# Four converted and five raw weight chunks in place of five and three, and a pool of their own for the bias tiles, in one decoder layer

## The chip, the cores and the metric

The kernel runs on one core of one Trainium2 chip, in one launch. The metric is the device time of one execution in microseconds, as the median of several runs. The profile shows the engines as PE (TensorE matmul), PEld (its weight load), DVE (VectorE), ACT (ScalarE), POOL (GpSimd) and SP (SyncE, which here only starts transfers).

## The reference

One layer of a decoder on 256 tokens of width 2048, all in float32:

```python
h  = rms_norm(x, norm_mix_pre)
c_q, c_kv, k_r, q_s, k_s, v_s, gates = split(h @ w_in)          # 2048 -> 7488
q  = rms_norm(c_q) @ w_q_up ; kv = rms_norm(c_kv) @ w_kv_up
A  = latent attention (16 heads, causal, rotary part)
B  = banded attention (32 query heads, 4 key heads, window 128,
     sinks, bias = rel_table[t5_bucket(distance)])
y  = (sigmoid(gA) * (A @ w_o_mla) + sigmoid(gB) * (B @ w_o_swa)) @ w_out
x  = x + rms_norm(y, norm_mix_post)
h  = rms_norm(x, norm_ffn_pre)
a, b = split(h @ w_up)                                           # 2048 -> 2 x 5632
y  = (gelu(causal_conv3(a)) * b) @ w_down
x  = x + rms_norm(y, norm_ffn_post)
```

## The kernel before

Every product of activations and weights is made of three matmuls on numbers split in a high and a low part (`fp32r`): high x high, high x low, low x high (`mm3`, L147 to L149, and the same in the FFN's first product at L977 and L981). The 256 tokens are two row blocks, t = 0 and t = 1.

The weights come in chunks of up to 1024 columns of a [128, 1024] tile, 512 KB each, 501 in all. A chunk has three steps (`wchunk`): SP loads it into a raw tile (L119), ACT copies it to the high part `whi` (L121), DVE subtracts that from the raw tile and gets the low part `wlo` (L122). Raw tiles come from a ring of `RAW` buffers (3) and are free when `wlo` is done; the pairs `whi`, `wlo` come from rings of `RING` buffers each (5) and are free when the last matmul has read them. So the load of chunk n waits for the `wlo` of chunk n - RAW, and the `whi` of chunk n for the matmuls of chunk n - RING. A tile takes 4 KB of each partition. A chunk may be given a pool of its own (`own`).

`gemm` runs over the chunks of one block of up to 512 output columns. With 512 columns a chunk holds two k-tiles, which makes 6 matmuls for each row block; with 256 columns it holds four k-tiles and makes 12 shorter ones for each. With `split=True` the matmuls of t = 1 are put aside in `todo` and run after those of t = 0 of the whole block, so that the work on the first rows can start while PE does the second rows. Then every chunk of the block stays converted until its turn in `todo`. This is used three times: in the last block of W_out (eight chunks, 229 to 236, the first three in a pool `px` with `EXTRA` = 3 buffers, the other five in the ring), in the first block of the FFN's product (chunks 237 to 244: one in pool `p8`, three in `px`, four in the ring), and in the last block of W_down (five chunks, 496 to 500, all in the ring).

Behind the last block of W_out stands `resid(t)`: the sum of squares (`yj`, `vy`), the inverse root in small steps (`ry`), `x2 = yg * ry + x2` (L840), transposes (`x2T`, L843) and the split into the FFN's input (`bhl`, L847 on ACT and L850 on DVE). Behind the last block of W_down stand `z_evac` (`z`, L1037 and `zj`, L1039) and `finish` (a root on ACT, L1054, and `ds`, L1062, with the stores) for each row block in turn.

The banded attention works in 16 units of two heads. Each loads its bias, 384 distances for each of two heads, from a strip in DRAM by two transfers of POOL (L425, L426) and adds it to the scores (L437, L438). Its queries come through `qx` (L203), transposes `xp` (L403) and a copy `x` (L406).

The order of the instructions on an engine is set by the Tile framework's scheduler at build time, with steps tied to the chunk number by `at` and `tick`; the first product's ACT, DVE and SP instructions stay in the order of the code. An engine takes its instructions in that order. Pools are taken from the on-chip memory one above the other: a pool that is opened after another was closed lies in the same place, and the first writer there waits for the last reader of what was there. `p1` takes the place of `p0`.

Of the kernel before, what the change touches and what calls it, by code (L numbers as in the profile page):

```python
# [19 lines left out]
P = 128  # L20
# [21 lines left out]
def trunk_layer(ctx, tc, x, x_cols_in, conv_cols_in, g_mix_post, g_ffn_post, w_in, w_q, w_kv,  # L42
# [4 lines left out]
    def open_pool(name, bufs=1, **kw):  # L47
        es = ExitStack()
        return es, es.enter_context(tc.tile_pool(name=name, bufs=bufs, **kw))
# [6 lines left out]
    base = ctx.enter_context(tc.tile_pool(name="base", bufs=1))  # L56
    ring = ctx.enter_context(tc.tile_pool(name="ring", bufs=RING))

    def sb(pl, shape, name, dt=F32, tag=None, bufs=None):
        return pl.tile(shape, dt, name=name, tag=tag or name, **({"bufs": bufs} if bufs else {}))  # L60
# [43 lines left out]
    def wchunk(src, shape, own=None, rawp=None, rbufs=1):  # L104
# [3 lines left out]
        raw = rawp.tile([P, 1024], F32, name=f"raw{i}", tag="xraw", bufs=rbufs) if rawp else \  # L108
            ring.tile([P, 1024], F32, name=f"raw{i}", tag="raw", bufs=RAW)
        dst = raw[:, :n]  # L110
# [26 lines left out]
    def drain():  # L137
        while steps:
            tick()
# [65 lines left out]


    esl, lpool = open_pool("lpool")
    es0, p0 = open_pool("p0")

    gx = sb(p0, [P, 38 + 256], "gx")  # L210
# [132 lines left out]
    es1, p1 = open_pool("p1")  # L343
# [72 lines left out]
    def swa_unit(u, t0):  # L416
# [3 lines left out]
        st = {}  # L420

        def load():
            st["bias"] = sb(p1, [P, 2, 384], f"bias{u}", tag="bias", bufs=2)
            row = lambda n: bass.AP(strip.tensor, strip.offset + h0 * 384, [[1, P], [384, 2], [1, n]])
            pool.dma_start(st["bias"][:, :, 0:256], row(256))  # L425
            pool.dma_start(st["bias"][:, :, 256:384], row(128))  # L426
            st["p"] = sb(p1, [P, 2, 384], f"p{u}", tag="p", bufs=3)
            st["mx"] = sb(p1, [P, 2, 2], f"mx{u}", tag="mx", bufs=3)
# [45 lines left out]
        def pv():  # L474
# [16 lines left out]
            pool.tensor_tensor(OL(u), st["o"], OH(u).bitcast(F32), op=ALU.subtract)  # L491

        at(t0 - (3 if u > 1 else 1), load)
        at(t0, lambda: score(0), lambda: score(1))
        at(t0 + 1, stats, lambda: expo(0), lambda: expo(1), norm)
# [99 lines left out]
    tb = {0: gate_b(0), 1: gate_b(1)}  # L595
    drain()
    es1.close()


    es2, p2 = open_pool("p2")  # L600
# [482 lines left out]
    es3.close()  # L1083


RING = 5
XCUT = [0, 1, 2, 3, 4, 6, 8, 10, 12, 14, 16]
X_LOAD = [0, 1, 2, 3, 4, 6, 7, 8, 10]
X_SQ = [4, 4, 5, 5, 6, 7, 8, 9, 10, 11]
# [3 lines left out]
LINE_B = 80  # L1093
LINE_W = 64
LINE_Z = 48
RAW = 3
STG = 4


# [61 lines left out]
```

## Time and profile before

| | |
|---|---|
| median of 3 runs | 1485.72 us (1485.46 to 1486.3) |
| the profiled execution: time | 1489.58 us |
| the profiled execution: span | 1487.8 us |
| mean granted TensorE clock | 0.997 |
| PE, DVE, ACT busy | 99%, 66%, 54% of the span |
| read from memory | 277.79 MB, 191 GB/s over the span |

The profile is of one execution on the one core; times in it are microseconds from the start of its span. A row of the timeline gives start, duration, engine, line, operation and tiles (without their numbers), and in brackets the idle time of the engine before it and what ended that. A row of the waits gives who waited for what: microseconds in all, times, the longest.

### The profile page before, as it was taken

To read this page: it belongs to the slowest core of one execution; us is meant where nothing else is said; L and a number is where in the kernel's file an instruction comes from. 1 tells how busy PE (TensorE), PEld (TensorE's weight loads), DVE (VectorE), ACT (ScalarE), POOL (GpSimd) and SP (SyncE) were. 2 spreads that over 40 slices of the span, in tenths; PEclk is the share of its full clock that TensorE was granted. 3 is DMA by queue.
4 is the path that set the end of the run, shared out by engine and by line. 5 is a ranking of instruction groups with operands and counts; after the bars stand their busy time and mean duration, and the time that the engine had idled before them with its cause. 6 is when DMAs were issued, how large, how long until landed. Compare 5 with 4: busy or idle time off the path is not lost.

```text
span 1487.8 us, 21191 instructions
## 1 busy us (share of the span) xinstructions
PE 1472.7 (99%) x7797; PEld 1263.0 (85%) x7797; DVE 979.4 (66%) x1711; ACT 806.0 (54%) x1336; POOL 57.9 (4%) x97
## 2 busy tenths in 40 slices
PE   9999999999999999999999999999999999999997
PEld 7788888888899988888888888888888888888887
DVE  7688884444667765555698776676444676677555
ACT  7588874434555554444566555554444555555443
POOL 0122210000000001000000000000000000000000
PEclk9999999999999999999999999999999999999999
DMA  8676656666655559766656666665556666665563
GB/s 268 191 192 156 166 174 199 211 206 206 184 157 162 164 162 307 245 216 201 198 171 184 198 187 183 198 187 189 191 196 197 187 185 191 190 189 184 194 196 114
DMA packets 162324, 285.52 MB, mean 192 GB/s; under 512 B 18555, under 2 KB 34844, under 8 KB 162092
## 3 DMA queue, kind: packets, MB, share of 16 engines
q1 hardware_dynamic: 157436, 268.39, 58.5%
q0 software_dynamic: 4784, 15.78, 4.2%
q8 instruction: 61, 1.00, 0.3%
q14 instruction: 43, 0.35, 0.1%
HBM read 277.79 MB, written 6.34 MB: 191 GB/s over the span
## 4 chain that ended last, share of the span: by engine, by line
PE 90%; ACT 3%; DMA 3%; DVE 3%; issue 1%; SPq 0%; DVEq 0%; ACTq 0%
PE accg L148 17%; PE accg L149 17%; PE accg L147 17%; PE ub L977 10%; PE ua L977 10%; PE ua L981 5%; PE ub L981 5%; DMA raw<-in_w_in_dram 3%; ACT whi L121 1%; ACT p L455 1%; DVE wlo L122 1%; PE mpo L730 1%; PE ms L696 1%; PE qn L659 1%; PE qn L660 1%
## 5 line engine op out<-in xcount | busy, mean ns | idle before, releaser
L122 DVE TENSOR_TENSOR wlo<-raw,whi 128x1024 fp32r<-128x1024 f32 (+2 forms) x501 | 608.6, 1217 | 421.3 <-ACT whi L121 420.1
L121 ACT CAST whi<-raw 128x1024 fp32r<-128x1024 f32 (+2 forms) x501 | 523.4, 1046 | 544.7 <-PE accg L149 305.7
L147 PE MATMUL accg<-whi,bhl 128*128 128x512 f32 (+1 forms) x608 | 230.9, 380 | 0.0
L149 PE MATMUL accg<-whi,bhl 128*128 128x512 f32 (+1 forms) x608 | 230.1, 378 | 0.0
L148 PE MATMUL accg<-wlo,bhl 128*128 128x512 f32 (+1 forms) x608 | 230.0, 378 | 0.0
L147 PE MATMUL accg<-whi,ahl 128*128 128x512 f32 (+1 forms) x544 | 213.3, 392 | 0.0
L148 PE MATMUL accg<-wlo,ahl 128*128 128x512 f32 (+1 forms) x544 | 210.9, 388 | 0.0
L149 PE MATMUL accg<-whi,ahl 128*128 128x512 f32 (+1 forms) x544 | 210.7, 387 | 0.0
L977 PE MATMUL ub<-ahl,whi 128*128 128x512 f32 x640 | 160.4, 392 | 0.0
L977 PE MATMUL ua<-ahl,whi 128*128 128x512 f32 x640 | 160.2, 392 | 0.0
L977 PEld LDWEIGHTS ua<-ahl,whi 128*128 128x128 f32 x640 | 115.7, 189 | 21.1
L977 PEld LDWEIGHTS ub<-ahl,whi 128*128 128x128 f32 x640 | 115.5, 189 | 21.1 <-ACT cc L897 0.2
L149 PEld LDWEIGHTS accg<-whi,bhl 128*128 128x128 f32 x608 | 114.4, 188 | 21.4
L148 PEld LDWEIGHTS accg<-wlo,bhl 128*128 128x128 f32 x608 | 114.4, 188 | 20.9
L147 PEld LDWEIGHTS accg<-whi,bhl 128*128 128x128 f32 x608 | 114.4, 188 | 20.9
L149 PEld LDWEIGHTS accg<-whi,ahl 128*128 128x128 f32 x544 | 102.4, 188 | 20.5
L147 PEld LDWEIGHTS accg<-whi,ahl 128*128 128x128 f32 x544 | 102.5, 188 | 18.0
L148 PEld LDWEIGHTS accg<-wlo,ahl 128*128 128x128 f32 x544 | 102.6, 189 | 17.7
L981 PEld LDWEIGHTS ub<-ahl,wlo 128*128 128x128 f32 x640 | 86.3, 191 | 5.6
L981 PEld LDWEIGHTS ua<-ahl,wlo 128*128 128x128 f32 x640 | 86.0, 191 | 5.5
L981 PE MATMUL ub<-ahl,wlo 128*128 128x256 f32 x640 | 88.0, 282 | 0.0
L981 PE MATMUL ua<-ahl,wlo 128*128 128x256 f32 x640 | 87.9, 282 | 0.0
(331 smaller groups left out, 1621.6 us busy)
## 6 DMA issues: line engine op xcount, KB each, us to landing
raw<-in_ffn_w_up_dram SPq DMA_DIRECT2D x176, 512.0 KB, 4.5
raw<-in_w_in_dram SPq DMA_DIRECT2D x111, 512.0 KB, 4.6
raw<-in_ffn_w_down_dram SPq DMA_DIRECT2D x88, 512.0 KB, 4.1
raw<-in_w_o_swa_dram SPq DMA_DIRECT2D x32, 512.0 KB, 3.9
raw<-in_w_o_mla_dram SPq DMA_DIRECT2D x32, 512.0 KB, 4.8
raw<-in_w_out_dram SPq DMA_DIRECT2D x32, 512.0 KB, 4.1
raw<-in_mla_w_q_up_dram SPq DMA_DIRECT2D x48, 128.0 KB, 2.7
bias<-strip POOLq DMA_DIRECT2D x16, 256.0 KB, 3.9
```

What stands on the lines that cost most here:

```text
L121: act.copy(hi[:, :n], raw[:, :n])
L122: vec.tensor_tensor(lo[:, :n], raw[:, :n], hi[:, :n].bitcast(F32), op=ALU.subtract)
L147: pe.matmul(o, ah, bh, start=start, stop=False)
L148: pe.matmul(o, ah, bl, start=False, stop=False)
L149: pe.matmul(o, al, bh, start=False, stop=stop)
L455: act.activation(pb[:, i, a:b], pb[:, i, a:b], AF.Exp, bias=st["nm"][:, i, t:t + 1], accum_out=st["sm"][:, i, t:t + 1])
L659: pe.matmul(o, wh, ch(k), start=k == 0, stop=False)
L660: pe.matmul(o, wh, cl(k), start=False, stop=False)
L696: pe.matmul(o, w, v_, start=n == 0, stop=False)
L730: pe.matmul(o, w(t), p_[:, c], start=n == 0, stop=n == 5)
L977: pe.matmul(acc[i], hi[:, c], hn[p][:, j * 512:(j + 1) * 512], start=p + j == 0, stop=stop)
L981: pe.matmul(acc[i][:, 0:256], lo[:, c], hn[p][:, j * 512:j * 512 + 256], start=False, stop=False)
```

## The change

Two sizes and one pool:

```diff
     esl, lpool = open_pool("lpool")
+    esb, pbias = open_pool("pbias")
     es0, p0 = open_pool("p0")
...
-            st["bias"] = sb(p1, [P, 2, 384], f"bias{u}", tag="bias", bufs=2)
+            st["bias"] = sb(pbias, [P, 2, 384], f"bias{u}", tag="bias", bufs=2)
...
     es1.close()
+    esb.close()
...
-RING = 5
+RING = 4
...
-RAW = 3
+RAW = 5
```

The ring of pairs loses one `whi` and one `wlo` tile (8 KB of a partition), the raw ring gains two tiles (8 KB). The two bias buffers (3 KB each) no longer lie in `p1`, above what `p0` held in the head, but in a place that nothing has used before. Lines after L207 move down by one, those after L598 by two.

The scheduler's order stays the same in nearly all places, with one difference throughout: where the conversion of chunk n + 1 stood, that of chunk n stands now. Three places differ by more or matter here.

ACT, in the head, ahead of the copy of the first transposed queries (`x20`; `qx`, `vx`, `kx` are the attention's queries, values and keys). Before:

```order
L121 CAST whi21_771<-raw21_769 128x1024
L121 CAST whi22_809<-raw22_807 128x1024
L200 CAST vx0_567<-vr0_615 128x4x64
L121 CAST whi23_863<-raw23_861 128x1024
L200 CAST vx1_568<-vr1_637 128x4x64
L200 CAST kx0_563<-kt0_641 128x384
L406 CAST x20_652<-xp0_647 128x512
L406 CAST x21_664<-xp1_659 128x512
```

ACT in the same place, after:

```order
L121 CAST whi20_723<-raw20_721 128x1024
L121 CAST whi21_774<-raw21_772 128x1024
L200 CAST vx0_570<-vr0_618 128x4x64
L121 CAST whi22_812<-raw22_810 128x1024
L200 CAST vx1_571<-vr1_640 128x4x64
L200 CAST kx0_566<-kt0_644 128x384
L407 CAST x20_655<-xp0_650 128x512
L407 CAST x21_667<-xp1_662 128x512
```

The last conversion ahead of `x20` is chunk 22's in place of chunk 23's; the rest is the same.

DVE, between W_out and the FFN, in the inverse root for the first rows (`vy0`, `ry0`), up to the first of `x2_0`. Before:

```order
L837 TENSOR_SCALAR vy0_7154<-vy0_7154 128x1
L179 TENSOR_SCALAR ry0_y_7157<-vy0_7154 128x1
L182 SCALAR_TENSOR_TENSOR ry0_t_7158<-vy0_7154,ry0_y_7157 128x1
L189 TENSOR_SCALAR ry0_t_7158<-ry0_t_7158 128x1
L190 TENSOR_TENSOR ry0_y_7157<-ry0_y_7157,ry0_t_7158 128x1
L182 SCALAR_TENSOR_TENSOR ry0_t_7158<-vy0_7154,ry0_y_7157 128x1
L122 TENSOR_TENSOR wlo238_7370<-raw238_7367,whi238_7369 128x1024
L192 TENSOR_SCALAR ry0_u_7159<-ry0_t_7158 128x1
L193 TENSOR_TENSOR ry0_u_7159<-ry0_u_7159,ry0_t_7158 128x1
L122 TENSOR_TENSOR wlo239_7382<-raw239_7379,whi239_7381 128x1024
L194 SCALAR_TENSOR_TENSOR ry0_y_7157<-ry0_u_7159,ry0_y_7157 128x1
L840 SCALAR_TENSOR_TENSOR x2_0_0_5855<-yg_0_0_6558,ry0_y_7157,x2_0_0_5855 128x512
```

DVE in the same place, after (eight more small steps of both rows, without a `wlo`, follow before `x2_0_0`):

```order
L828 TENSOR_TENSOR yg_0_3_6565<-accg_229_0_7057,gpost_5870 128x512
L839 TENSOR_SCALAR vy0_7158<-vy0_7158 128x1
L179 TENSOR_SCALAR ry0_y_7161<-vy0_7158 128x1
L122 TENSOR_TENSOR wlo242_7422<-raw242_7419,whi242_7421 128x1024
L182 SCALAR_TENSOR_TENSOR ry0_t_7162<-vy0_7158,ry0_y_7161 128x1
L122 TENSOR_TENSOR wlo243_7434<-raw243_7431,whi243_7433 128x1024
L189 TENSOR_SCALAR ry0_t_7162<-ry0_t_7162 128x1
L838 TENSOR_REDUCE vy1_7279<-ssy1_6571 128x1
L828 TENSOR_TENSOR yg_1_3_6569<-accg_229_1_7058,gpost_5870 128x512
L190 TENSOR_TENSOR ry0_y_7161<-ry0_y_7161,ry0_t_7162 128x1
L839 TENSOR_SCALAR vy1_7279<-vy1_7279 128x1
L122 TENSOR_TENSOR wlo244_7446<-raw244_7443,whi244_7445 128x1024
```

Three conversions of later chunks (242 to 244) now stand among these small steps in place of 238 and 239, and steps of the second rows (`vy1`, `yg_1_3`) as well. On PE, in the same place, the last six matmuls of t = 0, those of chunk 236, moved behind 30 and 34 of the 48 of t = 1.

PE, in the last block of W_down (`accg_496_0` is t = 0, `accg_496_1` is t = 1). Before:

```order
L147 MATMUL accg_496_0_13785<-whi500_13861,ghl9_7565 128x256
L148 MATMUL accg_496_0_13785<-wlo500_13862,ghl9_7565 128x256
L149 MATMUL accg_496_0_13785<-whi500_13861,ghl9_7565 128x256
L147 MATMUL accg_496_1_13786<-whi496_13789,bhl0_7556 128x256
L148 MATMUL accg_496_1_13786<-wlo496_13790,bhl0_7556 128x256
L149 MATMUL accg_496_1_13786<-whi496_13789,bhl0_7556 128x256
```

PE in the same block, after, with 22 matmuls of t = 1 ahead of the first row of chunk 500:

```order
L147 MATMUL accg_496_1_13790<-whi497_13811,bhl3_7563 128x256
L147 MATMUL accg_496_0_13789<-whi500_13865,ghl8_7568 128x256
L148 MATMUL accg_496_1_13790<-wlo497_13812,bhl3_7563 128x256
L149 MATMUL accg_496_1_13790<-whi497_13811,bhl3_7563 128x256
L147 MATMUL accg_496_1_13790<-whi498_13829,bhl4_7564 128x256
L148 MATMUL accg_496_1_13790<-wlo498_13830,bhl4_7564 128x256
L149 MATMUL accg_496_1_13790<-whi498_13829,bhl4_7564 128x256
L147 MATMUL accg_496_1_13790<-whi498_13829,bhl4_7564 128x256
L148 MATMUL accg_496_1_13790<-wlo498_13830,bhl4_7564 128x256
L149 MATMUL accg_496_1_13790<-whi498_13829,bhl4_7564 128x256
L147 MATMUL accg_496_1_13790<-whi498_13829,bhl5_7565 128x256
L148 MATMUL accg_496_0_13789<-wlo500_13866,ghl8_7568 128x256
```

Before, t = 1 follows when t = 0 is complete; now the twelve matmuls of chunk 500 for t = 0 stand in the middle of those of t = 1.

## The prediction

> **What bounds the kernel now.** I read the page's first lines, then the waits, then one window of the long middle.
>
> ```profile
> PE 1472.7 (99%) x7797; PEld 1263.0 (85%) x7797; DVE 979.4 (66%) x1711; ACT 806.0 (54%) x1336; POOL 57.9 (4%) x97
> PE 90%; ACT 3%; DMA 3%; DVE 3%; issue 1%; SPq 0%; DVEq 0%; ACTq 0%
> L122 DVE TENSOR_TENSOR wlo<-raw,whi 128x1024 fp32r<-128x1024 f32 (+2 forms) x501 | 608.6, 1217 | 421.3 <-ACT whi L121 420.1
> L121 ACT CAST whi<-raw 128x1024 fp32r<-128x1024 f32 (+2 forms) x501 | 523.4, 1046 | 544.7 <-PE accg L149 305.7
> ```
>
> PE is busy for 1472.7 of 1487.8 us, so all that can be won inside the span is about 15 us, and the change has to be priced where PE stands still or comes to stand still. The two conversions of a chunk take 1.05 us on ACT and 1.22 us on DVE.
>
> ```profile
> ACT whi L121 <- PE accg L149: 305.7, 198, 2.5
> ACT whi L121 <- DMA raw<-in_w_o_mla_dram: 29.3, 14, 4.1
> ACT whi L121 <- DMA raw<-in_w_in_dram: 24.1, 23, 3.9
> SPq L119 <- DVE wlo L122: 854.0, 360, 11.1
> 300.00:350.00 50.00, 50.00 (x222) 41.42 (x221) 23.25 (x20) 21.12 (x21) 1.08 (x2) 1.00 0.65 205
> ```
>
> ACT mostly waits for PE to give back a converted pair (305.7 us in 198 waits): the conversions run ahead as far as the ring lets them. Waits of ACT for the raw data are a sixth of that. The loads on SP wait 854.0 us for wlo, which frees a raw buffer. From 300 to 350 us PE is busy for 50.00 of 50.00 us (second number of the window's row), so none of these waits costs anything there. What counts is the few places where PE stops: the head, where the first weights come in, the handover from W_out to the FFN, and the end.
>
> **The steady stages: nothing.** A pair is freed four chunks ahead of its use with five pairs, and three ahead with four. A chunk is 12 matmuls of 512 columns; 48 such matmuls take the 10.88 us from 719.63 to 730.51 in the rows on the handover below, 0.227 us each, so a chunk is 2.72 us. The lead shrinks from 4 x 2.72 = 10.9 us to 8.2 us, of which the conversions need 1.05 + 1.22 = 2.3 us. About 5.9 us stay as cover for other work of ACT and DVE in between. The extra two raw buffers take away ACT's waits for raw data (29.3 and 24.1 us), which PE did not feel. Bounds: -2 us, if some of PE's 15 us without work goes with them, and +2 us, if in the banded attention, where ACT and DVE have most other work, the cover is used up once. I take 0.
>
> **The bias pool: nothing.** The first bias load no longer waits for what lay in that memory before, only for its source.
>
> ```profile
> POOL bias L425 <- DMA raw<-in_w_in_dram: 5.3, 1, 5.3
> 67.80 0.29 DVE L437 TENSOR_TENSOR p<-s,bias 128x128 f32<-128x128 f32 x1 [4.04 <-PE s L435]
> ```
>
> At most 5.3 us of waiting on POOL go, but the first reader, at 67.80, waited last for PE's scores and not for the bias. The scores hide it.
>
> **The head: a gain of 3.3 us.** Here a stall of PE does hang on the raw data.
>
> ```profile
> 54.69 1.05 ACT L121 CAST whi<-raw 128x1024 fp32r<-128x1024 f32 x1 [3.87 <-DMA raw<-in_w_in_dram]
> ...
> 60.66 1.04 ACT L121 CAST whi<-raw 128x1024 fp32r<-128x1024 f32 x1 [1.15 <-DMA raw<-in_w_in_dram]
> ...
> 62.24 0.60 ACT L406 CAST x<-xp 128x512 fp32r<-128x512 f32 x1
> 58.07 0.40 PE L149 MATMUL accg<-whi,ahl 128*128 128x512 f32 x1
> 60.46 0.40 PE L147 MATMUL accg<-whi,ahl 128*128 128x512 f32 x1
> 62.89 0.75 PE L403 MATMUL xp<-ident_r,qx 128*128 128x128 f32 x4 [2.03 <-ACT x L406]
> 63.44 0.76 PE L148 MATMUL accg<-wlo,ahl 128*128 128x512 f32 x1
> ...
> 66.11 0.39 PE L148 MATMUL accg<-wlo,ahl 128*128 128x512 f32 x1
> 64.00:66.00 2.00, 2.00 (x6) 1.61 (x5) 0.00 (x0) 0.27 (x1) 0.00 (x0) 0.50 0.91 271
> ```
>
> ACT takes its instructions in order. The x copy, for which PE stands still for 2.03 us, is behind the conversion at 60.66 (chunk 23), which waited 1.15 us for its load, as the one at 54.69 had waited 3.87. After the stall the granted clock is 0.50 (the third number from the end of the window's row, with the busy share of the DMA engines and the GB/s behind it), and from 63.44 to 66.11 six matmuls take 2.67 us in place of 6 x 0.227 = 1.36: another 1.3 us. With five raw buffers the load of chunk n waits for the wlo of chunk n-5 and no longer n-3, two conversions earlier, and with one pair less the conversion in that place of the row is chunk 22's. What gates it is the pair of chunk 18, whose last matmul is the one at 58.07, done at 58.5. So it starts 2.2 us earlier than 60.66. The x copy keeps its distance of 1.58 us: 60.1. The transposes at 62.89 follow 0.65 us behind it, at 60.7, where PE comes free at 60.9 (60.46 + 0.40). The stall goes, and the lower clock with it: -2.03 - 1.3 = -3.3. Bounds: 0, if the loads come no earlier because the DMA queues are what limits here (0.91 of them are busy from 64 to 66), and -3.6. I take the far end, since the gate that is left is a row of PE's and not a transfer.
>
> **The handover from W_out to the FFN: +5.9 us and something for the clock.** The last block of W_out runs all its matmuls for the first 128 rows (t0) and then those for the others (t1), so every chunk of it stays converted until its t1 matmuls come. Eight chunks, 229 to 236: three have buffers of their own, five fill the ring of five. In a ring of four, chunk 236 has to wait for chunk 232's t1.
>
> ```profile
> 719.63 0.39 PE L147 MATMUL accg<-whi,ahl 128*128 128x512 f32 x1
> ...
> 730.51 0.39 PE L147 MATMUL accg<-whi,ahl 128*128 128x512 f32 x1
> ...
> 736.89 1.34 PE L843 MATMUL x2T<-ident,x 128*128 128x128 f32 x8
> ...
> 743.80 0.39 PE L147 MATMUL accg<-whi,bhl 128*128 128x512 f32 x1
> 730.77 0.60 ACT L825 ACTIVATE yj<-accg 128x512 f32<-128x512 f32 x1 [3.88 <-PE accg L149]
> ...
> 732.07 1.05 ACT L121 CAST whi<-raw 128x1024 fp32r<-128x1024 f32 x1 [0.61 <-PE accg L149]
> ...
> 737.55 2.17 ACT L847 ACTIVATE bhl<-x2T,gmat 128x128 fp32r<-128x128 f32 x8 [1.70 <-PE x2T L843]
> 733.31 1.22 DVE L122 TENSOR_TENSOR wlo<-raw,whi 128x1024 fp32r<-128x1024 f32 x1
> ...
> 734.71 1.23 DVE L122 TENSOR_TENSOR wlo<-raw,whi 128x1024 fp32r<-128x1024 f32 x1
> ...
> 736.03 2.74 DVE L840 SCALAR_TENSOR_TENSOR x<-yg,ry_y,x 128x512 f32<-128x512 f32 x4
> ...
> 739.83 2.15 DVE L850 SCALAR_TENSOR_TENSOR bhl<-x2T,gmat,bhl 128x128 fp32r<-128x128 f32 x8
> ```
>
> Before, t0 is complete at 730.7 (yj at 730.77). The norm of its rows on DVE (two wlo stand in it), x at 736.03, the transposes at 736.89 and the splits behind them all run while PE does t1, and the FFN's first matmul at 743.80 waits for nothing. In the new order 42 matmuls of t0 are in a row, then t1 starts (719.63 + 42 x 0.227 = 729.15), and t0's last six stand behind 30 and 34 of t1's. Chunk 232 is free after t1's 24th, at 734.8 with its drain; whi 236 runs 734.8 to 735.9, wlo to 737.1, and t0 is complete at 738.5, or 7.8 us later. On DVE the norm of these rows now has three wlo in it (242, 243, 244), each behind a whi that waits for a pair that t1 still reads: 234 is free at 738.9, 235 at 740.3, 236 at 741.6. Adding 1.05 and 1.22 to these: wlo 242 ends at 741.5, 243 at 742.8, 244 at 744.9, and with the small steps left x starts at 745.65 and the first transposes at about 746.5. PE has no matmul left after 741.45 (48 + 48 done). The first k-tiles of the FFN's input, transposed, scaled and split, come at about 749.0, with eight more transposes (0.7 us) to do then: 749.0 + 0.7 - 743.80 = +5.9. If no wlo stood in that chain, the first transposes would come at 742.2 and the price would be +0.8: that is the lower bound. I take the upper one, since DVE can't overtake its own row.
>
> For the clock, the head's rows say that 2.03 us without work were followed by 0.50 until 66.11 and cost 1.3 us. Here PE is idle for about 5 us, cut by transposes of 128 columns, of which I can't say whether they keep the clock up. Between 0 and 1.3 I take the middle, +0.6. [...]
>
> **The tail: +2.9 us.** The last block of W_down is split in the same way and has five chunks, 496 to 500, all in the ring.
>
> ```profile
> 1464.60 0.28 PE L147 MATMUL accg<-whi,bhl 128*128 128x256 f32 x1
> ...
> 1471.80 0.28 PE L147 MATMUL accg<-whi,bhl 128*128 128x256 f32 x1
> ...
> 1478.88 0.28 PE L149 MATMUL accg<-whi,ghl 128*128 128x256 f32 x1
> 1464.80 1.05 ACT L121 CAST whi<-raw 128x1024 fp32r<-128x1024 f32 x1 [1.83 <-PE accg L149]
> ...
> 1473.05 1.28 ACT L1054 ACT_TABLE_LOAD   x1
> 1472.00 0.42 DVE L1037 TENSOR_TENSOR z<-ds,accg 128x256 f32<-128x256 f32 x1 [4.58 <-PE accg L149]
> ...
> 1475.51 2.74 DVE L1062 SCALAR_TENSOR_TENSOR ds<-ds,rz,x 128x512 f32<-128x512 f32 x4
> 1479.20 0.42 DVE L1037 TENSOR_TENSOR z<-ds,accg 128x256 f32<-128x256 f32 x1 [0.95 <-PE accg L149]
> ...
> 1481.36 2.74 DVE L1062 SCALAR_TENSOR_TENSOR ds<-ds,rz,x 128x512 f32<-128x512 f32 x4
> ```
>
> t0 and t1 are 60 matmuls of 0.12 us each (7.20 us from 1464.60 to 1471.80). Before, the first rows finish while t1 runs: z at 1472.00, table load, small steps, ds until 1478.25, and then DVE idles 0.95 us for t1. In the new order t0 stops after 48 (1470.36). whi 500 waits for chunk 496's t1 (12 matmuls, 1.44 us, and the drain: 1472.05), ends at 1473.1, wlo at 1474.4. t0's last eleven stand behind 31 of t1's and end at 1475.9, so z of the first rows comes 3.9 us later. The work behind it takes 1478.2 - 1472.0 = 6.2 us on DVE, and z of the other rows stands behind it: 1475.9 + 6.2 = 1482.1 in place of 1479.20, +2.9. All after that is one chain to the last store. PE's own end moves by 0.2 us at most. Bounds: 0, if t0 were no more than 0.95 us late, and +3.2.
>
> **Sum.** -3.3 + 5.9 + 0.6 + 2.9 = +6.1 us. The profiled execution's span is 1487.8 and its time 1489.58, 3.9 us above the runs' median; a difference carries over: 1485.72 + 6.1 = 1491.8 us.
>
> **The rivals.** (a) No difference that a measurement of this kernel can tell (within 0.2%, 2.97 us): the handover is cheap, +0.8, because the norm's small steps aren't held up by the three wlo. For it: with two wlo in it that norm still took only 5.3 us (730.77 to 736.03). Against it: the releases that these wlo now wait for lie behind t1. Time: 1485.72 - 3.3 + 0.8 + 2.9 = 1486.1.
> (b) Faster: the deeper raw ring is worth more than its place in the head. Of PE's 15 us without work some in the banded attention go too; with -3.3 in the head, -2 there, the handover at +0.8 and a tail of +1 it is 1482.2. It decides if the handover stays under about +1.3. Against it: the whole middle shows no idle PE, and the attention's short stalls are behind ACT and DVE rather than loads.
> (c) Slower by more: PE starves where cover is thinnest (+2, the bound above), the head gains nothing, or the clock falls fully: 1491.8 + 0.7 + 2 = 1494.5, and 1497.8 with no gain in the head.
>
> **Chances.** My case 0.60, (c) 0.16, (a) 0.14, (b) 0.10. Slower by over 0.2% (above 1488.7): mine and (c), 0.76. Faster (below 1482.7): 0.10. The range leaves out (b) and the worst of (c): 1485 to 1496. My case's own range is 1489 to 1494.
>
> **What would show it.** Right: PE's 2.03 us at 62.89 and the 0.50 clock behind it are gone; a PE stall of about 5 us shows just ahead of the FFN's first matmul with x2T waited for; yj of the first rows about 7.8 us later against the start of t1; the last z waits for DVE and not for PE. Wrong: no stall at the handover (then whi 236 got its pair earlier than I count), or stalls of PE on wlo in the banded attention.

## The result and the profile after

The changed kernel takes 1496.7 us (median of 4 executions, 1496.28 to 1496.94), the kernel before 1486.01 us (4 executions, 1485.46 to 1486.89): a ratio of 1.0071, 95% interval 1.0054 to 1.0089. That is 10.7 us more, where 6.1 were forecast and the range ended at 1496 us. The direction, the two places of the loss and most of their sizes came out; the gain in the head did not come, and the clock's term was too small.

First the head, in the timeline of the changed kernel (ACT, then PE), and the same place in a second profile of the kernel before, which has a span of 1484.3 us.

```profile
58.37 1.04 ACT L121 CAST whi<-raw 128x1024 fp32r<-128x1024 f32 x1 [1.81 <-PE accg L149]
...
59.95 0.60 ACT L407 CAST x<-xp 128x512 fp32r<-128x512 f32 x1
60.33 0.40 PE L147 MATMUL accg<-whi,ahl 128*128 128x512 f32 x1
60.61 0.53 PE L404 MATMUL xp<-ident_r,qx 128*128 128x128 f32 x4
```

```profile
58.57 1.05 ACT L121 CAST whi<-raw 128x1024 fp32r<-128x1024 f32 x1 [0.83 <-PE accg L149]
...
60.16 0.60 ACT L406 CAST x<-xp 128x512 fp32r<-128x512 f32 x1
60.49 0.40 PE L147 MATMUL accg<-whi,ahl 128*128 128x512 f32 x1
60.81 0.37 PE L403 MATMUL xp<-ident_r,qx 128*128 128x128 f32 x2
64.00:66.00 2.00, 2.00 (x18) 1.69 (x17) 1.68 (x8) 1.31 (x3) 0.00 (x0) 1.00 0.16 60
```

After the change the conversion ahead of the x copy waits for PE's pair, starts at 58.37 (58.5 was forecast), and PE runs through. But in the second profile of the kernel before it does so too: 58.57, waiting for PE, x at 60.16, the transposes right behind the matmul at 60.49, and a granted clock of 1.00 from 64 to 66. The stall that the prediction meant to win was not there to be won in that execution.

Then the handover, changed kernel: ACT, DVE and PE, and four windows (the granted clock is the third number from the end).

```profile
731.09 1.06 ACT L121 CAST whi<-raw 128x1024 fp32r<-128x1024 f32 x1 [0.30 <-PE accg L149]
...
734.97 0.60 ACT L827 ACTIVATE yj<-accg 128x512 f32<-128x512 f32 x1 [1.47 <-PE accg L149]
736.63 1.22 DVE L122 TENSOR_TENSOR wlo<-raw,whi 128x1024 fp32r<-128x1024 f32 x1
...
737.91 1.22 DVE L122 TENSOR_TENSOR wlo<-raw,whi 128x1024 fp32r<-128x1024 f32 x1
...
739.90 1.21 DVE L122 TENSOR_TENSOR wlo<-raw,whi 128x1024 fp32r<-128x1024 f32 x1
...
741.86 0.75 DVE L842 SCALAR_TENSOR_TENSOR x<-yg,ry_y,x 128x512 f32<-128x512 f32 x1
715.93 0.39 PE L147 MATMUL accg<-whi,ahl 128*128 128x512 f32 x1
...
742.71 1.94 PE L845 MATMUL x2T<-ident,x 128*128 128x128 f32 x8 [4.65 <-issue]
744.53 0.79 PE L147 MATMUL accg<-whi,bhl 128*128 128x512 f32 x1
...
747.05 0.63 PE L148 MATMUL accg<-wlo,bhl 128*128 128x512 f32 x1
740.00:742.00 2.00, 0.00 (x0) 0.00 (x0) 2.00 (x10) 0.00 (x0) 0.53 (x1) 0.53 0.85 249
742.00:744.00 2.00, 1.29 (x6) 1.20 (x7) 2.00 (x5) 1.23 (x3) 0.00 (x0) 0.50 0.99 304
...
748.00:750.00 2.00, 2.00 (x8) 1.64 (x7) 1.10 (x2) 0.98 (x5) 0.00 (x0) 0.50 0.08 29
750.00:752.00 2.00, 2.00 (x11) 1.60 (x10) 1.13 (x4) 1.50 (x7) 0.00 (x0) 0.91 0.00 0
```

W_out's last block begins at 715.93 (719.63 in the execution that the prediction read). The conversion of chunk 236 at 731.09 waits for PE, the sum of squares of the first rows (yj) follows at 734.97, the three subtractions stand in the norm's chain, and x starts at 741.86. PE, idle for 4.65 us, is then at half clock (0.50 in every window from 742 to 750) until about 750.

Last the tail, DVE of the changed kernel:

```profile
1480.80 0.42 DVE L1039 TENSOR_TENSOR z<-ds,accg 128x256 f32<-128x256 f32 x1 [1.68 <-PE accg L149]
...
1484.29 2.74 DVE L1064 SCALAR_TENSOR_TENSOR ds<-ds,rz,x 128x512 f32<-128x512 f32 x4
1486.95 0.41 DVE L1039 TENSOR_TENSOR z<-ds,accg 128x256 f32<-128x256 f32 x1
```

The second z has no wait in brackets any more: it stands behind the first rows' ds on DVE, where before it waited 0.95 us for PE.

How much each stretch costs can be read from the first matmul of W_out's last block and the first of W_down's last block. The second profile of the kernel before has these at

```profile
716.19 0.39 PE L147 MATMUL accg<-whi,ahl 128*128 128x512 f32 x1
...
1461.13 0.28 PE L147 MATMUL accg<-whi,bhl 128*128 128x256 f32 x1
```

and the changed kernel has the first at 715.93 (above) and the second at

```profile
1469.42 0.28 PE L147 MATMUL accg<-whi,bhl 128*128 128x256 f32 x1
```

Up to W_out's last block the changed kernel is 0.3 us ahead. From there to W_down's last block it takes 753.49 us in place of 744.94, which is 8.55 more, and from there to the end of the span 25.7 in place of 23.2, which is 2.5 more. Together that is 10.8, the difference of the two spans (1495.1 and 1484.3).

### The profile page after: what moved, and what is told of

Its sections match the earlier page's. It is cut to its first block, busy times and chain, and to the rows that moved or that the text cites. A ratio compares the mean times of both kernels' runs of the same rounds, so it can differ in the third digit from the quotient of the medians.

```text
span 1495.1 us, 21182 instructions
## 1 busy us (share of the span) xinstructions
PE 1474.7 (99%) x7797; PEld 1263.5 (85%) x7797; DVE 979.9 (66%) x1711; ACT 807.3 (54%) x1336; POOL 57.1 (4%) x97
## 4 chain that ended last, share of the span: by engine, by line
PE 93%; DVE 4%; ACT 2%; issue 1%; DMA 0%; SPq 0%; DVEq 0%; ACTq 0%
PE accg L149 17%; PE accg L147 17%; PE accg L148 17%; PE ub L979 10%; PE ua L979 10%; PE ua L983 5%; PE ub L983 5%; DVE wlo L122 1%; PE mpo L732 1%; PE ms L698 1%; ACT p L456 1%; PE qn L661 1%; PE qn L663 1%; PE qn L662 1%; PE acckv L148 0%
```

## The experiments

**The kernel before, again.** No edit.

> The unchanged kernel, profiled again. Theory A: the 2.03 us stall of PE in the head and the half clock behind it belonged to the one profiled execution that the prediction read, which was 3.9 us above the median of the runs; ordinary executions don't have them, so the change has nothing to win there. Then the span is about 1484 us (3.5 less than 1487.8), the conversion ahead of the x copy waits for no transfer, and PE runs through from 55 to 66 us at full clock. Theory B: every execution has the stall, and the 3.9 us are spread elsewhere: span near 1484 too, but with the 2.03 us and the clock of 0.50 at 64 us in it.

Measured: 1486.09 us, ratio 0.9998 (0.9988 to 1.0007). The profiled span is 1484.3 us, and all ten executions have spans between 1483.6 and 1484.9; 25 more of the same kernel on that chip lie between 1483.6 and 1485.5. The execution of the prediction (1487.8) is outside of all of them (the longest span of this kernel in any later run is 1486.8), and the rows above show the head without its stall. PE's rows of the two traces are together up to 58 us (the matmul at 58.07 stands at 58.09 here) and 3.4 us apart behind the stall (the `kt` transposes at 74.94 and 71.51), as they still are at W_out's last block (719.63 and 716.19). So the head makes nearly all of the 3.5 us by which that execution was longer, and theory A holds for these two. Two traces of later runs with the same rings, of the bias pool alone and of `EXTRA = 2` (both below), show a stall of 0.30 us and none in that place, at a granted clock of 1.00. Why the loads came later in the one execution is not shown, and of the executions without a trace only the spans are known.

**The handover's cause undone.** Chunk 236 gets a pair outside the ring; the FFN's first chunks trade places:

```diff
-extra={i: (px,) for i in range(EXTRA)} if last else None)
+extra={i: (px,) for i in range(EXTRA)} | {7: (p8,)} if last else None)
...
-first_extra = {0: (p8,)} | {i + 1: (px,) for i in range(EXTRA)}
+first_extra = {i: (px,) for i in range(EXTRA)} | {EXTRA: (p8,)}
```

> The changed kernel, with the handover's cause undone alone: chunk 236 gets the buffers of pool p8 and chunk 237 and 240 trade places with it, so that W_out's last block needs four pairs of the ring. The trace of the changed kernel puts the loss there at about 8.3 us (stall and clock). A: 1496.7 - 8.3 = 1488.4 us, PE's 48 matmuls of the first rows in a row and no stall ahead of the FFN. B (the handover's loss is only the forecast 6.5, the rest of the miss is elsewhere): 1490.2.

**The tail's cause undone.** The last block's fifth chunk uses two tiles that nobody reads any more:

```diff
+class Free:
+    def tile(self, shape, dt, name, tag):
+        return base.tile(shape, dt, name=name, tag="ahl0" if tag == "whi" else "ahl1")
...
-return gemm(xh, xl, w_down, k0, nk, c0, n, split=split, ps=ps)
+return gemm(xh, xl, w_down, k0, nk, c0, n, split=split, extra={4: (Free(),)} if split else None, ps=ps)
```

> The changed kernel, with the tail's cause undone alone: the fifth chunk of W_down's last block gets two tiles that nothing reads any more, so that the block needs four pairs of the ring. Both theories: 1496.7 - 2.9 = 1493.8 us, the last z waits for PE again. If it stays above 1495.7, the tail's term is under 1 us and its place is elsewhere.

**Both undone.** The two edits together.

> Both undone, so that the ring of four, the raw ring of five and the bias pool are left without a block that needs a fifth pair. A (nothing to win in the head): 1496.7 - 8.3 - 2.9 = 1485.5 us, the same as before within 1 us. B (the head's 3.3 us are won in every execution): 1482.7 us.

Measured: handover undone 1490.05 us (ratio to before 1.0027, 1.0018 to 1.0037), tail undone 1493.54 us (1.0047, 1.0032 to 1.0062), both 1487.17 us (1.0010, 1.0001 to 1.0020). Against 1496.7 that is -6.65, -3.2 and -9.5 us. The tail is near what was expected. Its four executions lie between 1492.07 and 1494.82 us, so the 3.2 is a rough figure; the step from the handover alone to both is 2.9. The last z waits for PE again (DVE, tail undone):

```profile
1484.88 0.42 DVE L1043 TENSOR_TENSOR z<-ds,accg 128x256 f32<-128x256 f32 x1 [0.95 <-PE accg L149]
```

The handover gives less than the 8.3 expected, and 1490.05 is the number that theory B gave. That is by chance. PE's timeline of that run shows why: no stall ahead of the FFN, the transposes between W_out's matmuls, but a new wait that the edit itself brought, since chunk 240 now waits for chunk 236's pair.

```profile
733.39 1.32 PE L845 MATMUL x2T<-ident,x 128*128 128x128 f32 x8
...
745.96 0.50 PE L148 MATMUL accg<-wlo,bhl 128*128 128x512 f32 x1 [1.24 <-DVE wlo L122]
```

With its 1.24 us the handover is worth 7.9 us by the medians, where the rows of the two blocks above gave 8.55; B's 6.5 is too little. The run with both undone has the same wait (1.23 us), which is most of the 1.7 us that it lies above A's 1485.5.

**Both undone, without that wait.** Pool p8 goes to the FFN's chunk 244 in place of 240:

```diff
-first_extra = {i: (px,) for i in range(EXTRA)} | {EXTRA: (p8,)}
+first_extra = {i: (px,) for i in range(EXTRA)} | {7: (p8,)}
```

> Both blocks undone as in the combined run, with a better place for the FFN's chunks: pool p8, which chunk 236 now uses, goes to chunk 244 (needed last) in place of 240, and 240 to 243 use the ring. The 1.23 us that PE waited for chunk 240's subtraction should go: 1487.2 - 1.2 to 1.6 = 1485.8 us, no difference from before (1486.0). If the deeper raw ring is worth something in ordinary executions once the blocks fit, it is below 1484; if the shorter ring costs something in the steady stages, it stays at 1487.

Measured: 1485.55 us against 1486.89 of before, ratio 0.9993 (0.9984 to 1.0002): no difference that is clear of the measurement, and about 11 us faster than the changed kernel. The wait is gone, as expected. With the ring of four, five raw tiles and the bias pool all in place, the steady stages cost and win nothing that could be told. A version that is shown to beat the kernel before was not found.

**Where the handover's loss comes from: the chain.** Three subtractions are put behind x2_0_0 on DVE by an order edge:

```diff
-vec.tensor_tensor(lo[:, :n], raw[:, :n], hi[:, :n].bitcast(F32), op=ALU.subtract)
+sub = vec.tensor_tensor(lo[:, :n], raw[:, :n], hi[:, :n].bitcast(F32), op=ALU.subtract)
+if (0, 3) in added and len(late) < 3 and id_in_block() >= 5:
+    late.append(sub)
+    tc.add_manual_dep(sub.ins, added[0, 0].ins.name, mybir.DependencyInfo(
+        mybir.DependencyClass.NoSync, mybir.DependencyReason.DATA), reason="behind x2_0_0")
...
-vec.scalar_tensor_tensor(x2[t][j], yg[t][j], r[:, 0:1], x2[t][j], op0=ALU.mult, op1=ALU.add)
+added[t, j] = vec.scalar_tensor_tensor(x2[t][j], yg[t][j], r[:, 0:1], x2[t][j], op0=ALU.mult, op1=ALU.add)
```

The condition picks chunks 242, 243 and 244. The edge sets the order on DVE only and adds no wait.

> The changed kernel with one order fixed: the subtractions of chunks 242, 243 and 244 on DVE are put behind the x2_0_0 of the handover; the late chunk 236 stays. If the handover's stall is made by these three in the norm's chain, x2_0_0 starts at about 738.1 in place of 741.86, the first transposes at about 739, PE's stall of 4.65 us falls to about 1 and the clock stays up: 1488.5 to 1491 us. If it is the late end of the first rows alone (yj at 734.97) that makes it, the time stays above 1495.

**Where it comes from: the clock.** PE gets other work while it waits:

```diff
             for f in todo:
                 f()
+            idle = pss.tile([P, 512], F32, name="idle", tag="s")
+            for i in range(NIDLE):
+                tc.keep_in_program_order(pe.matmul(idle, MH_(15)[:, P:2 * P], mth[7][:, :], start=True, stop=True))
...
+NIDLE = 19
```

> The changed kernel with 19 further matmuls of 512 columns on PE (4.3 us, their result is not used) right behind the last matmul of W_out, in the 4.65 us in which PE waits there. The wait itself stays. Theory A: the half clock behind the wait costs about 3 us (eleven FFN matmuls at 0.43 us or more in place of 0.23, and the transposes): 1493.7 us, and the granted clock stays 1.00 from 740 to 750. Theory B: behind the wait PE is held up by DVE's and ACT's splits and not by its clock: 1496.7 us, no change.

Measured: 1491.36 us for the chain (ratio 1.0034, 1.0021 to 1.0047), 1494.72 us for the clock (1.0058, 1.0043 to 1.0073). PE with the subtractions moved, and DVE's x:

```profile
738.29 1.42 DVE L851 SCALAR_TENSOR_TENSOR x<-yg,ry_y,x 128x512 f32<-128x512 f32 x2
739.14 1.34 PE L854 MATMUL x2T<-ident,x 128*128 128x128 f32 x8 [1.01 <-PE accg L158]
...
742.25 0.50 PE L158 MATMUL accg<-whi,bhl 128*128 128x512 f32 x1 [1.26 <-DVE ry_t L198]
```

The first stall is 1.01 us, as expected, and x starts at 738.29 in place of 741.86. A wait of 1.26 us for the splits is left behind it, so the gain is 5.3 us, and the time is 0.4 above the 1488.5 to 1491 expected. The late end of the first rows is only the smaller part; the subtractions in the norm's chain make the larger, with the clock that falls for it (0.50 from 742 to 750 in the changed kernel, 1.00 in every window from 736 to 752 here). One step of the second rows (yg, 0.68 us), which stood among the three, left the chain with them.

PE with the extra matmuls:

```profile
738.27 4.47 PE L881 MATMUL idle<-ahl 128*128 128x512 f32 x19
743.09 0.63 PE L845 MATMUL x2T<-ident,x 128*128 128x128 f32 x4 [0.35 <-PE idle L881]
...
744.40 0.47 PE L147 MATMUL accg<-whi,bhl 128*128 128x512 f32 x1
744.00:746.00 2.00, 1.49 (x8) 0.95 (x9) 2.00 (x7) 2.00 (x9) 0.00 (x0) 1.00 0.85 266
```

The transposes come 0.4 us later than without them, the FFN begins at 744.40 as it did at 744.53, the clock is 1.00, and 2.0 us are saved by the medians: neither the 3 that theory A put down nor the nothing of B. Between the first matmuls of the two blocks, W_out's last and W_down's last, it is 2.8 us (750.7 in place of 753.49), so half clock costs 2.0 to 2.8. Extra waits for the splits (1.49 of 2.00 us busy from 744 to 746) take some of what full clock gives.

**The other parts alone.** The bias pool with the old rings (`RING = 5`, `RAW = 3`), and the ring of four with three raw tiles (`RING = 4`, `RAW = 3`).

> The bias pool alone, rings of five pairs and three raw tiles as before. All theories: 1486.0 us, no difference beyond 1 us; the first bias load leaves a little earlier and nobody waits for it.

> The changed kernel with the raw ring left at three, so the ring of four pairs and the bias pool alone. A (the two more raw tiles win nothing in ordinary executions): 1496.7 us within 1 us. B (they win some of the head and of the attention's short stalls): 1499 us or more.

Measured: 1487.2 us for the bias pool (ratio 1.0004, 0.9995 to 1.0014), nothing that can be told, as expected. 1500.51 us for the ring of four alone (1.0097, 1.0082 to 1.0112), 3.8 us more than with five raw tiles: A is refuted here, the raw tiles do win something. Its trace shows it at the handover again (ACT, then PE):

```profile
737.48 1.05 ACT L121 CAST whi<-raw 128x1024 fp32r<-128x1024 f32 x1 [1.75 <-DMA raw<-in_ffn_w_up_dram]
738.43 0.59 ACT L827 ACTIVATE yj<-accg 128x512 f32<-128x512 f32 x1
746.74 1.94 PE L845 MATMUL x2T<-ident,x 128*128 128x128 f32 x8 [7.33 <-issue]
```

PE waits 7.33 us there and not 4.65. With three raw tiles the loads run less far ahead, ACT's conversions wait for their data as well, and the sum of squares of the first rows, which stands behind them on ACT, starts at 738.43 in place of 734.97. That execution has the shortest span of the four (1497.3; the longest 1500.3), and of what made the others longer there is no trace. Part of the 3.8 us stays open.

**The rule tried on the kernel before.** One edit, `EXTRA = 3` to `EXTRA = 2`, rings untouched:

> The kernel before, with one edit: EXTRA = 2 in place of 3, so that six chunks of W_out's last block share the ring of five. Rings and raw tiles as before, tail untouched. If the rule is that a split block must fit in its buffers, the handover alone breaks as in the changed kernel, with three raw tiles: chunk 236 comes after t1 has begun, the norm's chain has four subtractions in it, PE waits 4.5 to 7.5 us ahead of the FFN and the clock falls: 1486.2 + 8.5 to 11 = 1494.7 to 1497.2 us. If the loss needs the ring of four itself (less lead everywhere), it stays within 2 us of 1486.

Measured: 1494.47 us against 1485.87, ratio 1.0054 (1.0037 to 1.0071): +8.6 us with the ring of five, 0.2 below the range expected. PE and two windows of it:

```profile
744.45 1.94 PE L843 MATMUL x2T<-ident,x 128*128 128x128 f32 x8 [5.28 <-issue]
742.00:744.00 2.00, 0.00 (x0) 0.00 (x0) 2.00 (x10) 0.00 (x0) 0.00 (x0) 0.79 0.78 239
744.00:746.00 2.00, 1.55 (x8) 1.45 (x8) 2.00 (x7) 1.49 (x5) 0.00 (x0) 0.50 1.01 392
```

The same stall (5.28 us) and the same half clock (0.50 from 744 to 746). So what costs is not that the ring is shorter but that one block needs more pairs than it has.

## Why the prediction was wrong

The head: the step that failed. The rows were read rightly, and the changed kernel does just what they said (58.37 against 58.5 for the conversion, no stall, full clock). But "a difference carries over" was false for this term. The sum took 3.3 us off the median of the runs for a stall that the profiled execution had and that no later trace of these rings shows beyond 0.30 us; the gap of 3.9 us between that execution and the median, which the prediction itself set down, was for the most part this stall. Against the second profile the changed kernel wins 0.3 us up to W_out's last block. Without the term the sum is 5.9 + 0.6 + 2.9 = +9.4, a time of 1495.1 us inside the range.

The clock: 0.6 us was taken between 0 and 1.3; it measured 2.0 to 2.8. The bound was the mis-sized part. It came from a stall of 2.03 us, after which half clock (0.50) lasted for six matmuls; behind the longer stall it lasted from the transposes at 742.71 to about 750.4 (a mean of 0.91 from 750 to 752), 5.8 us after the FFN's first matmul.

The handover's stall: right. The handover's 7.9 us less the clock's 2.0 leaves 5.9 by the medians, and 8.55 less 2.8 leaves 5.7 by the rows; 5.9 was forecast. Counted from the start of the block, which is 3.7 us earlier than in the execution that the prediction read, the forecast 738.5 for the first rows' end becomes 734.8 (yj at 734.97), 745.65 for x becomes 741.95 (741.86), and 746.5 for the transposes 742.8 (742.71). DVE's order decided it, as argued: with the subtractions moved, 5.3 us went. Two things in the working were off. Adding 1.05 and 1.22 to the times at which the pairs come free gives 741.2, 742.6 and 743.9 for the three subtractions' ends, and not the 741.5, 742.8 and 744.9 that it goes on with; the trace has the later ones (737.85, 739.13 and 741.11, plus 3.7). ACT does the sums of squares of both row blocks (at 734.97 and 738.16) ahead of these conversions, a term that the working does not name. And the lower bound, +0.8 without subtractions in the chain, was too low: with them moved the kernel is still 4.96 us above the one before (1491.36 and 1486.40), which is over 2 us more than the tail's share.

The tail: right. +2.9 was forecast, 3.2 and 2.9 came off by undoing it, and DVE's z is bound by ds as said: it starts 17.53 us behind the block's first matmul (1469.42 to 1486.95), where before it was 14.60, +2.9. At the end of the span 2.5 of that are left.

The steady stages and the bias pool: right at nothing. From 200 to 700 us PE is busy for all of the 500 us in both kernels:

```profile
200.00:700.00 500.00, 500.00 (x2613) 428.15 (x2613) 295.24 (x428) 241.56 (x344) 18.05 (x33) 1.00 0.65 202
```

(changed kernel), and the version with both blocks mended is level with before. The bias pool alone made no difference either.

Of the rivals, (c), slower by more, is the one that came in two of its three parts: "the head gains nothing" (3.3 us) and "the clock falls fully", which cost more than the 0.7 it was given. The third, 2 us of PE starving where cover is thinnest, is seen nowhere. (a) and (b) needed a cheap handover, which it was not.

## What to carry to other kernels

Before a stall in a profile is put down as a gain, see whether the profiled execution is as fast as the others. Where it is slower by about the stall's size, the stall is the likely reason, and a second profile of the same kernel settles it.

A ring's depth is not set by the steady stages alone: count, for each block that holds its chunks back, how many it holds at once. One too many costs here 3 us at the end and 8 us where a norm's chain follows, and a deeper raw ring only softens it (3.8 us here between three and five raw tiles, part of it unexplained).

In an engine's fixed order a background operation inside a chain of small steps brings its own wait into that chain. Three subtractions of 1.2 us cost 5.3 us that way, the clock's fall included, and putting them behind the chain's end got that back without any more memory.

## What was not expected of the hardware

How long PE may be idle before its clock falls was not constant. In the changed kernel PE's last matmul ends at 738.06 (742.71 - 4.65), and the mean clock of 0.53 from 740 to 742 puts the fall at about 740.1, 2.1 us later. In the kernel with `EXTRA = 2` the last matmul ends at 739.17, and 0.79 from 742 to 744 puts it at about 743.2, 4.0 us later. These times, and those below, are estimates from the windows' means, with 1.00 on one side of the change and 0.50 on the other, as the windows beside them show in the head, in the changed kernel and with `EXTRA = 2`. With stalls of 1.01 and 1.26 us, 2 us apart (the subtractions moved), the clock did not fall at all: it is 1.00 in every window from 736 to 752.

Stalls of the same length differ in it too. With the tail undone the stall is the same as in the changed kernel (PE stops at 739.15 and starts at 743.81), but the clock falls only behind its end, 5.0 us after PE stopped (two windows of that run):

```profile
744.00:745.00 1.00, 0.94 (x6) 0.58 (x5) 1.00 (x3) 0.93 (x3) 0.00 (x0) 0.58 0.52 221
...
750.00:751.00 1.00, 1.00 (x5) 0.90 (x4) 0.20 (x1) 0.48 (x2) 0.00 (x0) 0.51 0.01 4
```

By these it was at half from 744.16 to 750.98, 6.8 us. In the same way it is 3.4 us in the head that the prediction read (62.66 to 66.08, the fall 1.8 us after PE stopped at 60.86; 0.83 from 62 to 63, 0.96 from 66 to 67), 10.2 us in the changed kernel (740.1 to 750.4) and 6.8 us with `EXTRA = 2` (743.2 to 750.0; 0.58 from 743 to 744, 0.51 from 749 to 750). In these four traces the longer times are close to two and three times the shortest. What sets the moment of the fall, and what brings the clock back, they do not settle.
